# Hybrid mLSTM / neighbourhood-attention layer on one core: loading keys and queries four steps sooner, and weight splits ahead of the first tile's pieces

## The chip, the cores and the metric

The kernel runs on one core of a Trainium2 chip. The metric is the time of one execution on the device in microseconds (us), the median of several runs. Inputs and weights are in HBM, all in fp32.

## The reference

One layer over 2048 tokens of width 1024. Three token mixers run on one RMS-normalised input; their outputs are projected, gated, merged and added to the residual stream; an MLP with squared ReLU follows.

```python
def hybrid_layer(x, mem, ...):
    h = rmsnorm(x, g_mix)
    z = h @ w_in                                  # 1024 x 5648
    qk_m, v_m, o_m, i_pre, f_pre, qkv_na, q_mem, gate_pre = jnp.split(z, ...)
    # 1. bidirectional chunkwise mLSTM on conv(qk_m), v_m and the gates
    # 2. neighbourhood attention: 32 x 64 grid, window 8 x 16, 8 heads of 32
    h_na = neighbourhood_attention(rmsnorm(q_na), rmsnorm(k_na), v_na, rpb)
    # 3. cross-attention into 256 memory tokens
    h_mem = memory_cross_attention(q_mem, rmsnorm(mem, g_mem), w_mem_kv, ...)
    y = gates[0]*(h_m @ w_proj_mlstm) + gates[1]*(h_na @ w_proj_na) + gates[2]*(h_mem @ w_proj_mem)
    x = x + y @ w_out
    u = rmsnorm(x, g_ffn) @ w_up
    return x + jnp.square(jax.nn.relu(u)) @ w_down
```

## The kernel before

**Products.** Every large product is made of three fp32r matmuls (`mm3`, L242 to L244): each operand is kept as a high part and a low part, and high x high, high x low and low x high are summed in PSUM. A weight unit of 512 KB is loaded into a raw tile (`wr`, three buffers, issued by SP), then split: ScalarE writes the high part (L185), VectorE the low part (L186), into one of five `ws` buffers. `take` fetches units some steps ahead of their use (`self.ahead`, 5). `self.later` moves the splits of a unit back in the scheduler's order.

**Stages.** Phase 1 goes over four blocks of 512 tokens. It projects the normalised input `hT` to everything that the mixers need, and runs both attentions beside it. Phase 2 runs the mLSTM beside the gate projections. Phase 3 merges, projects and does the MLP. The order on TensorE is written out by hand; the other engines' orders come from a list scheduler that goes by priority. `queued(marks)` lets the instructions inside it be scheduled only behind the marked instructions.

**The beginning.** `mem_setup` projects the 256 memory tokens (PSUM tiles `mx`, weights from the first four units). While it runs, the first token tiles are loaded and normalised: ScalarE squares a tile of 128 x 1024 (L350), GpSimd makes the reciprocal root (L335, L336), VectorE scales (L352). TensorE then transposes a tile in two groups of four squares (L358, PSUM tiles `tr`), and each of the eight pieces is evicted twice into `hT`: ScalarE writes the high part (L363), VectorE the low part (L364). The first block has its four tiles in the order 2, 3, 0, 1; here they are called the first to the fourth tile. A tile's projection to neighbourhood queries and keys (PSUM `mm`, evicted as `zna`, L522) is eight steps of three matmuls; step k needs piece k of the tile, and the weight unit of steps 2i and 2i+1. The units of the first tile are called here the first to the fourth. The first tile's transposes run inside the projection of the memory tokens, those of the others inside the projection of the tile ahead of each: after its fourth and sixth step in the first tile, after the second and fourth in the second and third.

Beside this, `rms_x` (L462) squares the four tiles of the next block on ScalarE, `mem_rms` the memory tokens, `na_qk` (L964 to L971) normalises the keys and queries of a tile with VectorE and GpSimd, and GpSimd's result for the memory tokens is used by VectorE in L1232 and L1233.

**Key and query loads.** Neighbourhood attention works on units (four token rows, a group of four heads, a half of the columns). The two halves of a pair share the tiles `naq` and `nak`, two buffers each. `na_load_qk` issues six loads for a pair on SP (L1064, L1065), and is called by `na_unit` when the first half of the pair is set up, which happens as soon as the unit before it has done its first head (one head per step). Scores of a head are one matmul, L1110.

Of the kernel before, what the change touches and what calls it, by code (L numbers as in the profile page):

```python
# [16 lines left out]
AF = mybir.ActivationFunctionType  # L17
# [5 lines left out]
D = 1024  # L23
# [16 lines left out]
WSP, WRAW, AHEAD = 5, 3, 5  # L40
# [43 lines left out]
class Body:  # L84
    def __init__(self, tc, a):
        self.tc, self.nc, self.a = tc, tc.nc, a
        self.n = 0
        self.later, self.ahead = LATER, AHEAD
        self.streams, self.qkq, self.memq, self.aux_end = [], [], [], False
        self.na_ready, self.na_end, self.na_rate, self.tk = [], False, 1, 0  # L90
        self.na_v, self.na_vfree, self.scored = [], 2, False
        self.jobs, self.out, self.split = [], (), ()
        self.wplan, self.wready = self.plan(), []

# [905 lines left out]
    def na_stream(self):  # L1000


        todo, fetched, prev, ready = [], [], [], []
        biases, freed = [], [0] * NAB
        cur = last = None
        late = False
        while True:
            while self.na_ready:
                g = self.na_ready.pop(0)
                todo += [(g, hg, half) for hg in range(2) for half in range(2)]  # L1010
            if todo and not fetched and (cur is None or cur["h"] > 0):
                last = self.na_unit(*todo.pop(0), last, 4 if cur else 8)
                fetched.append(last)
                biases += [(last, h) for h in range(4)]
            if cur is None and not fetched and self.na_end and not prev and not ready:
                return
            if self.tk % 2:
                due = ready.pop(0)[1] if ready and ready[0][0] >= NA_VALUES and not self.scored else None
                if due and (self.na_rate == 2 or late):
                    self.na_values(due)  # L1020
                    due, late = None, False
                late = bool(ready and ready[0][0] >= NA_VALUES)
                self.scored = False
                step = self.tk == 3 or self.na_rate == 2
                if step and prev and prev[0][0] >= NA_LATER:
                    u, h, sb = prev.pop(0)[1]
                    self.na_transpose(u, h, sb)
                    if h == 3:
                        ready.append([0, u])
                if due:  # L1030
                    self.na_values(due)
                if step:
                    if cur is None and fetched and fetched[0]["wait"] <= 0:
                        cur = fetched.pop(0)
                    if cur:
                        while len(cur["bias"]) <= cur["h"]:
                            self.na_bias(*biases.pop(0))
                            freed.pop(0)
                        freed.append(3)
                        prev.append([0, self.na_scores(cur, cur["h"])])  # L1040
                        cur["h"] += 1
                        if cur["h"] == 4:
                            cur = None
            for u in fetched:
                u["wait"] -= 1
            for x in prev + ready:
                x[0] += 1

            freed = [max(n - 1, 0) for n in freed]
            if biases and freed and not freed[0]:  # L1050
                self.na_bias(*biases.pop(0))
                freed.pop(0)
            yield

    def na_load_qk(self, g, hg, kr0, nr):
        nc = self.nc
        q = self.p_a.tile([96, 4, 256], F32R, name=f"naq{g}_{hg}", tag="naq", bufs=2)
        k = self.p_a.tile([96, 4, 11 * 64], F32R, name=f"nak{g}_{hg}", tag="nak", bufs=2)
        qs = self.scr["qs"][:, g, hg].rearrange("(h d) l f t -> d h l (f t)", d=32)
        ks = self.scr["ks"][:, hg, :, kr0 * 64:(kr0 + nr) * 64].rearrange("(h d) l t -> d h l t", d=32)  # L1060

        for i, (lq, lk) in enumerate(((0, 0), (0, 1), (1, 0))):
            ds = slice(32 * i, 32 * i + 32)
            nc.sync.dma_start(q[ds].bitcast(F32), qs[:, :, lq])  # L1064
            nc.sync.dma_start(k[ds, :, :nr * 64].bitcast(F32), ks[:, :, lk])  # L1065
        return q, k

    def na_unit(self, g, hg, half, before, wait):

        nc = self.nc  # L1070
        kr0 = min(max(4 * g - 4, 0), 24)
        nr = 8 if g in (0, 7) else 11
        u = dict(g=g, hg=hg, half=half, nk=nr * 40, pts=[], h=0, wait=wait)
        u["qk"] = before["qk"] if half else self.na_load_qk(g, hg, kr0, nr)
        u["kts"] = [(3 * i, min(3, nr - 3 * i)) for i in range((nr + 2) // 3)]
        u["ho"] = before["ho"] if half else self.t("nho", [128, 2, 256], 1, F32R)
        u["bias"] = []
        self.na_v.append(u)
        self.na_load_v()
        return u  # L1080
# [75 lines left out]
    def mem_setup(self):  # L1156
        nc, a, p_a = self.nc, self.a, self.p_a


        warm = self.ps("mx")  # L1160
        for _ in range(9):
            nc.tensor.matmul(warm[:, 0:128], self.ones, self.ones, start=True, stop=True)
        gm = p_a.tile([128, 8], F32, name="gmem")
        self.gmix = p_a.tile([128, 8], F32, name="gmix")
        nc.scalar.dma_start(gm, a["g_mem"])
        mT = p_a.tile([128, 4 * 704], F32, name="memT", tag="nak", bufs=2)[:, :2 * D].rearrange("p (k t) -> p k t", k=8)
        later, self.later = self.later, 0
        for k in range(0, 8, 2):
            if k == 0:
                self.fetch(2)  # L1170
            (nc.sync if k else nc.scalar).dma_start(mT[:, k:k + 2], a["memT"][k * 128:(k + 2) * 128].rearrange("(k p) t -> p k t", p=128))
            for i in (k, k + 1):
                hi, lo, g = self.hT[:, 0, i, 0:256], self.hT[:, 1, i, 0:256], gm[:, i:i + 1]
                nc.scalar.activation(hi, mT[:, i], AF.Copy, scale=g)
                nc.vector.scalar_tensor_tensor(lo, mT[:, i], g, hi.bitcast(F32), ALU.mult, ALU.subtract)
            if k:
                self.fetch()
            if k == 2:
                nc.sync.dma_start(self.gmix, a["gT_mix"])
                self.prep_x()  # L1180
        self.prep_x()
        self.later = 0
        with self.queued(self.square):
            self.fetch()
        first = self.split
        self.later = 120
        self.fetch()
        second = self.split
        w = self.take(4)
        self.later = later  # L1190
        xs = p_a.tile([128, 4 * 704], F32, name="xstage", tag="nak", bufs=2)
        gq = p_a.tile([128, 2], F32, name="gmqk_raw")
        nc.sync.dma_start(gq, a["g_mem_qk"])
        self.gmqk = p_a.tile([128, 2], F32, name="gmqk")
        nc.vector.tensor_scalar(self.gmqk[:, 0:1], gq[:, 0:1], 0.125, None, ALU.mult)
        nc.vector.tensor_copy(self.gmqk[:, 1:2], gq[:, 1:2])
        self.mk = p_a.tile([128, 2, 2, 256], F32R, name="mk")
        self.mv = p_a.tile([128, 2, 256], F32, name="mv")
        ps = [self.ps("mx") for _ in range(2)]
        self.trans_x(MEM_T)  # L1200
        turns = self.jobs[-2:]

        def turn(f, marks):
            with self.queued(marks()):
                f()
        self.jobs[-2:] = [lambda f=f: turn(f, lambda: first) for f in turns]
        self.jobs += [lambda i=i: turn(lambda: self.prep_x(xt=xs[:, i * D:(i + 1) * D]), lambda: self.turned + second) for i in range(2)]
        for k in range(8):
            wk = w[k // 2]
            for t in range(2):  # L1210
                self.mm3(ps[t], self.lhs_tok(self.hT, k, t), (wk[:, 0, k % 2], wk[:, 1, k % 2]), k == 0, k == 7)
            self.tick()
        self.memz = []
        for t, p in enumerate(ps):
            z = self.t("zm", [128, 256], 4)
            nc.scalar.activation(z, p[:, 0:256], AF.Copy)
            nc.vector.tensor_copy(self.mv[:, t], p[:, 256:512])
            self.memz.append(z)

    def mem_rms(self):  # L1220
# [468 lines left out]
```

## Time and profile before

| what | value |
|---|---|
| median of 3 runs | 2863.81 us (2863.42 to 2864.61) |
| the profiled execution's own time | 2865.11 us |
| its span, first to last instruction | 2863.4 us |
| TensorE busy | 2844.4 us, 99% of the span |
| VectorE, ScalarE, GpSimd busy | 2046.7, 1163.9, 199.0 us |
| mean granted TensorE clock | 0.999 |

Times in the profile are microseconds from the span's start; PE is TensorE, DVE VectorE, ACT ScalarE, POOL GpSimd, SP the engine that issues most DMAs (SPq its queue). A row of the timeline gives start, duration, engine, line, operation, tile written and tiles read, the count, and in brackets how long the engine sat idle before it and what ended that. A row of the waits gives the total, the number of times and the longest.

### The profile page before, as it was taken

The numbers are of one execution on the slowest core, as the hardware profiler recorded it, in microseconds if no ns is written. First come the engines' busy times: TensorE is split into PE (matmuls) and PEld (weight loads), VectorE is DVE, ScalarE is ACT, GpSimd is POOL, SyncE is SP. The second block draws the span as 40 slices with busy tenths as digits, with TensorE's granted clock in tenths as the row PEclk, the third lists the DMA queues.
The fourth block names the chain that finished last, engine by engine and source line by source line (L and its number), as shares of the span: only waits on it lengthen the run. The fifth ranks groups of instructions, "written<-read, shape, count | busy, mean of one in ns | idle before, by whom it ended". The sixth has DMA issues, their size and how long they took to land.

```text
span 2863.4 us, 41480 instructions
## 1 busy us (share of the span) xinstructions
PE 2844.4 (99%) x14950; PEld 2355.7 (82%) x14950; DVE 2046.7 (71%) x3522; ACT 1163.9 (41%) x2205; POOL 199.0 (7%) x254
## 2 busy tenths in 40 slices
PE   9999999999999999999999999999999999999999
PEld 7888888888887888888888888888888888888887
DVE  7686865477765555647699888866786998887666
ACT  6464654355544433532343334333223433343331
POOL 3221210011000122310000000000000000000000
PEclk9999999999999999999999999999999999999999
DMA  8686777886899888977444447756773444476553
GB/s 294 210 281 208 248 238 245 263 245 204 281 312 310 266 271 265 308 262 267 121 152 149 149 162 244 242 196 229 256 219 121 152 149 149 162 249 230 196 188 133
DMA packets 345149, 631.70 MB, mean 221 GB/s; under 512 B 29584, under 2 KB 151376, under 8 KB 344944
## 3 DMA queue, kind: packets, MB, share of 16 engines
q1 hardware_dynamic: 344528, 628.79, 66.9%
q8 instruction: 118, 1.93, 0.3%
q14 instruction: 87, 0.71, 0.1%
q10 hardware_dynamic: 416, 0.27, 0.0%
HBM read 452.32 MB, written 176.62 MB: 220 GB/s over the span
## 4 chain that ended last, share of the span: by engine, by line
PE 92%; DVE 3%; DMA 2%; issue 1%; ACT 1%; POOL 0%; SPq 0%; ACTq 0%; DVEq 0%; POOLq 0%
PE mm L242 28%; PE mm L244 27%; PE mm L243 27%; PE tr L1130 2%; DMA wr<-in_w_units_dram 1%; PE pn L902 1%; PE mx L1144 1%; PE mx L1110 1%; PE pn L905 1%; PE mx L911 1%; PE mx L1305 1%; PE tr L1295 1%; PE mx L1275 1%; DVE ws L186 0%; DVE cy L707 0%
## 5 line engine op out<-in xcount | busy, mean ns | idle before, releaser
L242 PE MATMUL mm<-X,ws 128*128 128x512 f32 x896 | 349.5, 390 | 0.2 <-ACT u L1499 0.2
L243 PE MATMUL mm<-X,ws 128*128 128x512 f32 x896 | 348.6, 389 | 0.0
L244 PE MATMUL mm<-X,ws 128*128 128x512 f32 x896 | 348.6, 389 | 0.0
L186 DVE TENSOR_TENSOR ws<-wr,ws 128x1024 fp32r<-128x1024 f32 (+2 forms) x195 | 237.5, 1225 | 124.3 <-ACT ws L185 122.7
L242 PE MATMUL mm<-hT,ws 128*128 128x512 f32 (+1 forms) x776 | 304.8, 393 | 1.4 <-DMA hT<-s_hT 1.4
L244 PE MATMUL mm<-hT,ws 128*128 128x512 f32 (+1 forms) x776 | 301.7, 389 | 0.0
L243 PE MATMUL mm<-hT,ws 128*128 128x512 f32 (+1 forms) x776 | 301.4, 388 | 0.0
L185 ACT ACTIVATE ws<-wr 128x1024 fp32r<-128x1024 f32 (+2 forms) x195 | 204.6, 1055 | 192.6 <-PE mm L244 135.7
L244 PE MATMUL mm<-X 128*128 128x512 f32 x616 | 239.7, 389 | 0.5 <-DVE X L1563 0.5
L242 PE MATMUL mm<-X 128*128 128x512 f32 x616 | 239.7, 389 | 0.0
L243 PE MATMUL mm<-X 128*128 128x512 f32 x616 | 239.6, 389 | 0.0
L242 PE MATMUL mm<-ws,hT 128*128 128x512 f32 (+2 forms) x640 | 226.4, 354 | 2.7 <-ACT ws L185 1.6
L212 ACT ACTIVATE ws<-wr 128x512 fp32r<-128x512 f32 x224 | 133.9, 627 | 232.8 <-PE mm L244 145.6
L243 PE MATMUL mm<-ws,hT 128*128 128x512 f32 (+2 forms) x640 | 223.3, 349 | 2.1 <-DVE ws L186 2.1
L244 PE MATMUL mm<-ws,hT 128*128 128x512 f32 (+2 forms) x640 | 223.6, 349 | 0.1
L1562 ACT ACTIVATE X<-X 128x1024 fp32r<-128x1024 f32 x109 | 115.7, 1062 | 209.4 <-DMA X<-s_s 92.5
L242 PEld LDWEIGHTS mm<-X,ws 128*128 128x128 f32 x896 | 168.2, 188 | 36.0 <-ACT u L1499 0.6
L243 PEld LDWEIGHTS mm<-X,ws 128*128 128x128 f32 x896 | 168.2, 188 | 35.3 <-issue 0.5
L244 PEld LDWEIGHTS mm<-X,ws 128*128 128x128 f32 x896 | 168.2, 188 | 34.8
L1579 DVE TENSOR_TENSOR acc<-acc,mm 128x512 f32<-128x512 f32 x192 | 126.3, 682 | 70.0 <-PE mm L244 70.0
L1563 DVE TENSOR_TENSOR X<-X 128x1024 fp32r<-128x1024 f32 x109 | 132.4, 1222 | 58.0 <-ACT X L1562 57.4
L242 PEld LDWEIGHTS mm<-hT,ws 128*128 128x128 f32 x776 | 146.1, 188 | 31.0 <-issue 2.8
(280 smaller groups left out, 5946.1 us busy)
## 6 DMA issues: line engine op xcount, KB each, us to landing
wr<-in_w_units_dram SPq DMA_DIRECT2D x289, 512.0 KB
s_s<-u SPq DMA_DIRECT2D x32, 1024.0 KB
s_g<-ev SPq DMA_DIRECT2D x96, 256.0 KB
ev<-s_g SPq DMA_DIRECT2D x96, 256.0 KB
s_a<-u SPq DMA_DIRECT2D x96, 256.0 KB
X<-s_s SPq DMA_DIRECT2D x45, 512.0 KB
nab<-in_rpb_dram SPq DMA_DIRECT2D x96, 220.0 KB
xt<-in_w_units_dram SPq DMA_DIRECT2D x32, 512.0 KB
```

The source lines that it names most:

```text
L185: s = nc.scalar.activation(w[:, 0, ks], raw[:, ks], AF.Copy)
L186: v = nc.vector.tensor_tensor(w[:, 1, ks], raw[:, ks], w[:, 0, ks].bitcast(F32), ALU.subtract)
L212: nc.scalar.activation(hi, src, AF.Copy)
L242: mm(out, lhs[0], rhs[0], start=first, stop=False)
L243: mm(out, lhs[0], rhs[1], start=False, stop=False)
L244: mm(out, lhs[1], rhs[0], start=False, stop=last)
L902: mm(pn[h % 2][:, h // 2], pt[:, h], v1[:, h], start=h < 2, stop=first)
L905: mm(pn[h % 2][:, h // 2], qw[hp, h // 2], C[hp, h // 2], start=False, stop=True)
L1130: nc.tensor.transpose(ptp[0:120, j], sb[:, j * 120:(j + 1) * 120], self.ident)
L1562: nc.scalar.activation(hi, src, AF.Copy)
L1563: nc.vector.tensor_tensor(lo, src, hi.bitcast(F32), ALU.subtract)
L1579: nc.vector.tensor_tensor(c, first[t] if first else c, p, ALU.add)
```

## The change

Two parts. First, the key and query loads of the next pair are issued as soon as the first half of the present pair has done its first head, and kept in a table until its unit is set up; before, they were issued when the second half of the present pair had done its first head. That is four heads, or four steps, sooner.

Second, in `mem_setup`: the split of the sixth unit (the second of the first token tile) comes behind the split of the fifth in the scheduler's order; the pieces of the first token tile come behind both; `self.ahead` is 3 there, so that the two units after these are not fetched at this place; one of them is fetched in the middle of the projection, behind the first tile's pieces; the squares of the third and fourth tile come behind that unit's split; and the evictions of the memory projection (`zm`, `mv`) come behind the first tile's pieces. Nothing is computed otherwise, and the order on TensorE stays as it was.

```diff
@@ na_stream
+            nxt = [x for x in todo if x[2] == 0][:1]
+            if nxt and nxt[0] not in self.na_keys and cur and not cur["half"] and cur["h"] > 0:
+                self.na_keys[nxt[0]] = self.na_load_qk(*nxt[0][:2])
             if todo and not fetched and (cur is None or cur["h"] > 0):
                 last = self.na_unit(*todo.pop(0), last, 4 if cur else 8)
@@ na_unit
-        u["qk"] = before["qk"] if half else self.na_load_qk(g, hg, kr0, nr)
+        u["qk"] = before["qk"] if half else self.na_keys.pop((g, hg, half), None) or self.na_load_qk(g, hg)
@@ mem_setup
         first = self.split
         self.later = 120
-        self.fetch()
+        with self.queued(first):
+            self.fetch()
         second = self.split
+        self.ahead = 3
         w = self.take(4)
+        self.ahead = AHEAD
         self.later = later
...
-        turns = self.jobs[-2:]
+        turns, marks = self.jobs[-2:], list(first + second)
...
-        self.jobs[-2:] = [lambda f=f: turn(f, lambda: first) for f in turns]
-        self.jobs += [lambda i=i: turn(lambda: self.prep_x(xt=xs[:, i * D:(i + 1) * D]), lambda: self.turned + second) for i in range(2)]
+        self.jobs[-2:] = [lambda f=f: turn(f, lambda: marks) for f in turns]
+        preps = [lambda i=i: self.prep_x(xt=xs[:, i * D:(i + 1) * D]) for i in range(2)]
+        def last():
+            turn(turns[1], lambda: marks)
+            turn(self.fetch, lambda: self.turned)
+            marks.extend(self.turned + self.split)
+        self.jobs[-1:] = [last]
+        self.jobs += [lambda f=f: turn(f, lambda: marks) for f in preps]
@@ mem_setup, the evictions of the memory projection
-            nc.scalar.activation(z, p[:, 0:256], AF.Copy)
-            nc.vector.tensor_copy(self.mv[:, t], p[:, 256:512])
+            with self.queued(self.turned):
+                nc.scalar.activation(z, p[:, 0:256], AF.Copy)
+                nc.vector.tensor_copy(self.mv[:, t], p[:, 256:512])
```

Three stretches of the orders show what moves. The first is ScalarE around the last piece of the first token tile. Before (`tr_380` holds pieces of the first tile, here its last one, `tr_474` of the second; `ws_296`, `ws_301` and `ws_306` are the second to fourth unit, `ws_311` is a unit for later; `xstage` are the squares of the third and fourth tile):

```order
L363 ACTIVATE hT<-tr_380,gmix 128x128
L185 ACTIVATE ws_296<-wr_295 128x2x512
L350 ACTIVATE ev_400,sm_401<-xstage 128x1024
L185 ACTIVATE ws_301<-wr_300 128x2x512
L350 ACTIVATE ev_461,sm_462<-xstage 128x1024
L363 ACTIVATE hT<-tr_474,gmix 128x128
L185 ACTIVATE ws_306<-wr_305 128x2x512
```

And now, from the same last piece on, ScalarE (`tr_370` holds it, `tr_474` and `tr_493` the second tile's pieces, `ws_384` is the fourth unit and `ws_429` the one for later; ahead of these rows stand the splits of the second and, after the first two pieces, of the third unit):

```order
L363 ACTIVATE hT<-tr_370,gmix 128x128
L1230 ACTIVATE zm_402<-mx_313 128x256
L1230 ACTIVATE zm_405<-mx_314 128x256
L185 ACTIVATE ws_384<-wr_383 128x2x512
L350 ACTIVATE ev_395,sm_396<-xstage 128x1024
L350 ACTIVATE ev_461,sm_462<-xstage 128x1024
L363 ACTIVATE hT<-tr_474,gmix 128x128
L363 ACTIVATE hT<-tr_493,gmix 128x128
L185 ACTIVATE ws_429<-wr_428 128x8x128
```

All splits of the first tile's units now stand ahead of the two squares, and both squares stand ahead of every piece of the second tile.

The second place is ScalarE at the fourth tile (`tr_581` and `tr_600` hold its pieces, `xt_768` and `xt_784` are the third and fourth tile of the next block, squared by `rms_x`). Before, the square of `xt_784` stood behind the fourth tile's last piece (the second row here) and three weight splits:

```order
L462 ACTIVATE xt_768,sm_716<-xt_768 128x1024
L363 ACTIVATE hT<-tr_600,gmix 128x128
L522 ACTIVATE zna_626<-mm_574 128x512
L964 ACTIVATE sq_677<-zna_572 128x512
L185 ACTIVATE ws_434<-wr_433 128x8x128
L185 ACTIVATE ws_439<-wr_438 128x8x128
L1244 ACTIVATE sq_686<-zm_407 128x4x64
L185 ACTIVATE ws_444<-wr_443 128x8x128
L462 ACTIVATE xt_784,sm_716<-xt_784 128x1024
```

Now the two squares stand close to each other on ScalarE:

```order
L363 ACTIVATE hT<-tr_581,gmix 128x128
L462 ACTIVATE xt_768,sm_716<-xt_768 128x1024
L363 ACTIVATE hT<-tr_581,gmix 128x128
L363 ACTIVATE hT<-tr_600,gmix 128x128
L462 ACTIVATE xt_784,sm_716<-xt_784 128x1024
```

Both squares now stand inside the fourth tile's pieces, ahead of five of the eight.

The third place is SP at the last pair of neighbourhood units. Before, its loads stood behind the values (`nav_0_1`) and the last bias (`nab_0_1_3`) of the unit before it:

```order
L182 DMA wr_9747<-in_w_units_dram 128x1024
L1094 DMA nav_0_1_9856<-s_vna 120x2x128
L1095 DMA nav_0_1_9856<-s_vna 80x128
L105 DMA s_hna<-nho_9194 256x1x256
L1101 DMA nab_0_1_3_9878<-in_rpb_dram 128x320
L1064 DMA naq_1_9886<-s_qs 32x4x256
L1065 DMA nak_1_9887<-s_ks 32x4x512
```

Now they stand behind the last bias of the half before that one (`nab_0_0_3`), and ahead of a weight unit:

```order
L1105 DMA nab_0_0_3_9711<-in_rpb_dram 128x320
L1069 DMA naq_1_9719<-s_qs 32x4x256
L1070 DMA nak_1_9720<-s_ks 32x4x512
L1069 DMA naq_1_9719<-s_qs 32x4x256
L1070 DMA nak_1_9720<-s_ks 32x4x512
L1069 DMA naq_1_9719<-s_qs 32x4x256
L1070 DMA nak_1_9720<-s_ks 32x4x512
L182 DMA wr_9654<-in_w_units_dram 128x1024
```

The six loads moved up in SP's queue past four biases, two value loads, two weight units, two loads for the sums of down weights and five stores.

More of the change, by code (lines that the diff above doesn't have):

```diff
@@ L90, in __init__ @@
         self.na_ready, self.na_end, self.na_rate, self.tk = [], False, 1, 0
-        self.na_v, self.na_vfree, self.scored = [], 2, False
+        self.na_v, self.na_vfree, self.scored, self.na_keys = [], 2, False, {}
         self.jobs, self.out, self.split = [], (), ()
@@ L1053, in na_stream, with na_load_qk @@
             yield
-    def na_load_qk(self, g, hg, kr0, nr):
+    def na_load_qk(self, g, hg):
         nc = self.nc
+        kr0 = min(max(4 * g - 4, 0), 24)
+        nr = 8 if g in (0, 7) else 11
         q = self.p_a.tile([96, 4, 256], F32R, name=f"naq{g}_{hg}", tag="naq", bufs=2)
@@ L1070, in na_unit @@
         nc = self.nc
-        kr0 = min(max(4 * g - 4, 0), 24)
         nr = 8 if g in (0, 7) else 11
         u = dict(g=g, hg=hg, half=half, nk=nr * 40, pts=[], h=0, wait=wait)
-        u["qk"] = before["qk"] if half else self.na_load_qk(g, hg, kr0, nr)
+        u["qk"] = before["qk"] if half else self.na_keys.pop((g, hg, half), None) or self.na_load_qk(g, hg)
         u["kts"] = [(3 * i, min(3, nr - 3 * i)) for i in range((nr + 2) // 3)]
```

## The prediction

> **What bounds the kernel now.** I read the page first, then the waits of TensorE, the timeline of the places where it waits, and the windows by stretch. The page's head says who sets the end.
>
> ```profile
> span 2863.4 us, 41480 instructions
> PE 2844.4 (99%) x14950; PEld 2355.7 (82%) x14950; DVE 2046.7 (71%) x3522; ACT 1163.9 (41%) x2205; POOL 199.0 (7%) x254
> ```
>
> TensorE is busy for all but 19.0 us of the span, so a change that adds no matmul and takes none away can only win what TensorE waits. The waits of TensorE, longest in total first (total, times, longest), are 13 rows:
>
> ```profile
> PE mm L243 <- DVE ws L186: 2.1, 3, 0.8
> PE mx L1110 <- DMA nak<-s_ks: 1.7, 1, 1.7
> PE mm L242 <- ACT ws L185: 1.6, 1, 1.6
> ...
> PE mm L242 <- ACT zif L546: 1.0, 2, 0.8
> ...
> PE mm L242 <- ACT u L1499: 0.2, 1, 0.2
> ```
>
> They sum to 13.6 us. The change aims at the second row (one load of keys) and at the first and third (splits that the first token tile waits for). Where these stand, by the timeline of TensorE:
>
> ```profile
> 20.57 0.39 PE L242 MATMUL mm<-ws,hT 128*128 128x512 f32 x1
> 23.68 0.49 PE L242 MATMUL mm<-ws,hT 128*128 128x512 f32 x1 [1.59 <-ACT ws L185]
> 24.94 0.80 PE L243 MATMUL mm<-ws,hT 128*128 128x512 f32 x1 [0.77 <-DVE ws L186]
> 30.77 0.50 PE L243 MATMUL mm<-ws,hT 128*128 128x512 f32 x1 [0.61 <-DVE ws L186]
> 91.29 0.39 PE L242 MATMUL mm<-ws,hT 128*128 128x272 f32 x1 [0.84 <-ACT zif L546]
> ```
>
> The first three waits, 2.97 us, lie in the first token tile. What that tile loses in all is seen in the windows, one row for each of the four tiles of the first block, then three for the stretch of conv and values:
>
> ```profile
> 20.57:32.04 11.47, 8.50 (x34) 6.22 (x32) 9.20 (x21) 9.26 (x20) 2.10 (x4) 0.85 0.60 190
> 32.04:38.45 6.41, 6.41 (x33) 5.29 (x32) 3.44 (x10) 5.58 (x14) 3.98 (x3) 1.00 1.02 393
> 38.45:45.25 6.80, 6.68 (x34) 5.21 (x33) 3.97 (x14) 5.16 (x14) 1.07 (x3) 1.00 0.51 162
> 45.25:50.69 5.44, 5.44 (x25) 4.46 (x24) 3.41 (x7) 5.44 (x11) 1.81 (x2) 1.00 0.91 311
> 60.00:70.00 10.00, 10.00 (x49) 8.27 (x48) 9.36 (x17) 3.43 (x7) 2.72 (x4) 1.00 0.99 331
> 70.00:80.00 10.00, 10.00 (x67) 9.25 (x67) 9.89 (x17) 5.28 (x10) 5.58 (x2) 1.00 0.94 296
> 80.00:90.00 10.00, 9.83 (x76) 9.08 (x75) 9.96 (x26) 3.76 (x10) 6.23 (x5) 1.00 0.62 205
> ```
>
> The columns are the stretch, its length, busy time of PE, PEld, DVE, ACT and POOL, the granted clock, the DMA share and GB/s. The fourth tile (24 matmuls, no transposes) takes 5.44, that is 0.227 a matmul; the second, with two groups of transposes, 6.41, so I count 0.4 for a group. The first takes 11.47: 5.06 more than the second, the waits and a clock of 0.85. But ScalarE is busy 25.4 of these 30.1 us. Moving its work about frees little of it, and TensorE needs each tile's pieces from it.
>
> **The change part by part.** *Keys.* The rows of the last pair: two heads of the half before, the last key load on SP's queue, and the wait.
>
> ```profile
> 848.35 0.39 PE L1110 MATMUL mx<-nak,naq 96*128 96x320 f32 x1
> 851.58 0.40 PE L1110 MATMUL mx<-nak,naq 96*128 96x320 f32 x1
> 853.21 0.43 SPq L1065 DMA_DIRECT2D nak<-s_ks  x1
> 860.90 0.38 PE L1110 MATMUL mx<-nak,naq 96*128 96x320 f32 x1 [1.70 <-DMA nak<-s_ks]
> ```
>
> A head takes 3.23, so four steps are 12.9 us: the load, which took 7.7 us from issue to use, would be in some 11 us early. The six loads go ahead of a weight unit on SP; that unit's turn comes about six issues of 0.43 later, 2.6 us, covered by units fetched five ahead. The gain lies between 0 (another transfer is late next) and 1.7; I take **1.7**, since no other scores wait for their keys in the trace.
>
> *First token tile.* Durations and landings:
>
> ```profile
> 2.17 0.47 SPq L182 DMA_DIRECT2D wr<-in_w_units_dram  x1
> 8.09 1.06 ACT L185 ACTIVATE ws<-wr 128x1024 fp32r<-128x1024 f32 x1 [1.10 <-DMA wr<-in_w_units_dram]
> 14.25 2.25 SPq L182 DMA_DIRECT2D wr<-in_w_units_dram  x2
> 15.85 1.06 ACT L185 ACTIVATE ws<-wr 128x1024 fp32r<-128x1024 f32 x1
> 23.66 1.23 DVE L186 TENSOR_TENSOR ws<-wr,ws 128x1024 fp32r<-128x1024 f32 x1 [0.47 <-ACT ws L185]
> 44.28 0.62 ACT L363 ACTIVATE hT<-tr,gmix 128x128 fp32r<-128x128 f32 x2 [0.16 <-DVE hT L364]
> 45.06 0.62 ACT L363 ACTIVATE hT<-tr,gmix 128x128 fp32r<-128x128 f32 x2 [0.16 <-DVE hT L364]
> ```
>
> The second unit is issued at 14.25; its split can start no sooner than 16.9, the end of the first unit's, and no later than 20.2 (5.92 from issue to use, as in the upper rows). I take 18.7. Then ScalarE has it at 19.8, VectorE at 21.0; the first pieces follow (lower half 21.3, its partner 21.5); the third unit's lower half ends at 22.7; and the other pieces, which alternate between ScalarE and VectorE at 0.78 a pair, end their lower halves at 22.9, 23.7 and 24.5. TensorE comes at 20.57, waits for these four, and ends the fourth step at 24.75. Two groups of transposes and twelve matmuls later, and 0.1 for the fourth unit's lower half (27.1), the tile ends at **28.4** instead of 32.04.
>
> *Second tile.* ScalarE goes on with the evictions of the memory projection, the fourth split (to 25.9) and two squares before any piece.
>
> ```profile
> 23.53 1.05 ACT L350 ACTIVATE ev<-xstage 128x1024 bf16<-128x1024 f32 x1
> 25.61 0.75 DVE L352 TENSOR_SCALAR xstage<-xstage,rs 128x1024 f32<-128x1024 f32 x1 [0.72 <-ACT ws L185]
> 33.53 0.69 DVE L966 TENSOR_REDUCE sm<-sq 128x16 f32<-128x512 f32 x1 [0.47 <-ACT sq L964]
> 39.73 0.35 DVE L1232 TENSOR_SCALAR zm<-zm,rs 128x256 f32<-128x256 f32 x1 [2.65 <-POOL rs L336]
> ```
>
> From a square's start to its scaling are 2.08. The second square starts at 26.9, so its scaling on VectorE runs from 29.0 to 29.7, and the first pieces' lower halves, behind it there, end at 30.0; a split for later (1.23) stands before the next, 31.7. Behind these, ScalarE has an eviction, a square of the memory tokens and the square for L966 between the pieces, so I have the fourth step's lower half at 34.9. TensorE, which came at 28.4, ends that step at 35.2, and the tile at 35.2 + 0.4 + 12 x 0.227 = **38.3**: the 3.6 us have gone to the second tile.
>
> *Third and fourth tile.* The chain from L966 over GpSimd to L1232 took 6.2 before; L966 now starts at 34.0, so L1232 at 40.2, 0.5 later than before, and two of the third tile's pieces stand behind it in VectorE's order as they did. That tile ends at about 45.5 (before 45.25). In the fourth, two squares stand ahead of five of its pieces.
>
> ```profile
> 42.06 1.89 SPq L482 DMA_DIRECT2D xt<-in_x_dram  x2
> 51.02 1.06 ACT L462 ACTIVATE xt<-xt 128x1024 f32<-128x1024 f32 x1
> ```
>
> The second was done at 51.02. Its load waits for the buffer that the square before it frees, at 42.5 by my count; with 3.7 us to land (I had 4.4 for the second weight unit, and the queue is emptier) its square runs at 46.2 to 47.3, the pieces of the third and fourth step come at 47.9 and 48.7, and the tile ends at 48.95 + 2.72 = **51.7**, 1.0 later than the 50.69 of before. Bounds: no loss if the load is in by 45, and with the 7.7 us that the key load took a tile end of 55.7, 5.0 later.
>
> *Conv and values, 50 to 92 us.* VectorE is busy 9.36, 9.89 and 9.96 of each 10 us there, and its backlog makes the waits of 0.17 and 0.84 (the L546 row, 1.0). Two of its waits ahead of this stretch shorten, since GpSimd now makes the next block's root ahead of a key norm:
>
> ```profile
> 55.48 0.69 DVE L471 TENSOR_TENSOR zna<-ident,rs 128x512 f32<-128x512 f32 x1 [2.28 <-POOL rs L336]
> 90.61 0.41 DVE L545 COPY zm<-mm 128x256 f32<-128x256 f32 x1
> ```
>
> So VectorE reaches L545 about 1 us sooner, TensorE gets there later, and both waits go; with the restart after each I count **1.3**. Bounds are 0 and 1.6.
>
> *The sum:* 1.0 later at the fourth tile, less 1.3, less 1.7: **2.0 us less**. The rest of phase 1 and part of phase 2 get other orders on SP, ScalarE and VectorE; TensorE's own order is the same. I bound what that does by the largest single wait of the table on each side, 1.7, and take nothing. The profiled execution takes 2865.11, 1.7 outside its span, and 1.3 more than the median; 2.0 off gives 2863.1 there, and **2861.8** as median.
>
> On the clock: in the first tile 0.85 was granted over a stretch in which TensorE's longest wait was 1.59. The Trainium skill, TensorE: Matmul & The Clock Gate, section on the HAM clock gate, says the clock halves after an idle window of about 3.4 us. The trace differs, since no wait here is so long and the clock fell. By the rule no wait of the changed start would slow the clock, and the sum stays; by the trace it may, but the tiles then wait for pieces anyway.
>
> **The rivals.** *The start's gain stays.* If the pieces of the second tile come in time (the squares land early in ScalarE's idle time, 4.7 us over these four tiles), the 3.6 us are kept, and VectorE's later stretch, fed sooner, moves with them: 3.6 + 1.0 (the L546 row) + 1.7 = 6.3 less, 2858.8 and as median 2857.5. For it speaks that the waits named are real; against it, the two squares ahead of all pieces.
>
> *Slower: the last square's load.* If that load takes as long as the key load did, TensorE is 5.0 late at the fourth tile; less 1.3 and 1.7 that is 2.0 more, 2867.1 and as median 2865.8. It decides from a landing at 48.2 on, 2.0 after the one I counted, where the sum of -2.0 is used up. For it: before, the square came at 51.02 and nothing shows when the load was in.
>
> *The key loads don't help.* They go sooner but the transfers that they pass on SP come late and hold TensorE as long: 0.3 less, 2863.5 as median. For it, two weight units are among the transfers passed; against it, units are fetched five ahead.
>
> **How the numbers follow.** Chances: forecast 0.50, start kept 0.22, slower 0.15, keys without gain 0.13. A measurement of this kernel can tell 0.2%, 5.7 us, from no change: faster needs less than 2858.1. That holds for a little over half of the second case, 0.13; slower needs over 2869.5, which only the far end of the third reaches, 0.04; the rest, 0.83, is within. The range reaches from a little beyond the second case to the third: 2856.8 to 2866.2.
>
> **What would show it.** Right: no wait at L1110; the first tile ends near 28.4 with waits below 1 us in its first four steps; TensorE waits for pieces (L363, L364) in the second tile and ahead of the fourth tile's third step; conv starts between 50.5 and 52; no wait for L546 near 90. Wrong: conv starts at 47 to 48 (the second case), or after 53 (the third); a new wait of over 2 us anywhere behind 100 us would break the sum.

## The result, and the profile after

| | before | after |
|---|---|---|
| median | 2863.96 us (2863.42 to 2865.30, 5 runs) | 2890.18 us (2889.35 to 2892.23, 5 runs) |
| ratio after to before | 1 | 1.009, 95% interval 1.0078 to 1.0101 |
| profiled execution's own time | 2865.11 us | 2890.5 us |
| its span, mean granted clock | 2863.4 us, 0.999 | 2888.8 us, 0.996 |

The kernel became slower by 26 us. The page's head after, span and engines:

```profile
span 2888.8 us, 41484 instructions
PE 2854.4 (99%) x14950; PEld 2361.0 (82%) x14950; DVE 2045.0 (71%) x3522; ACT 1163.3 (40%) x2205; POOL 203.2 (7%) x254
```

The same matmuls stand there in the same order, and VectorE and ScalarE have no more work than before. TensorE is busy 10.0 us longer, and the span holds 15.4 us more in which it isn't. Since TensorE's order is the same, each matmul can be set beside its twin and the lag read. It is 0.9 us at 92.5, 4.9 behind the site at 163, 8.5 behind 314, 14.1 behind 591, 17.1 behind 772, 18.7 behind 812, 17.6 at 878 (where the wait for keys is gone), 19.5 behind 884, 25.9 behind 946 and 25.9 at the end. So nearly all of it comes up between 95 and 960 us, at seven sites. The windows of that stretch (busy time of PE, PEld, DVE, ACT, POOL, then granted clock, DMA share, GB/s), before:

```profile
95.00:960.00 865.00, 860.52 (x5560) 717.05 (x5559) 573.35 (x1286) 441.98 (x938) 87.14 (x91) 1.00 0.80 256
```

and after:

```profile
95.00:960.00 865.00, 843.73 (x5443) 702.55 (x5442) 560.63 (x1268) 433.19 (x926) 91.75 (x93) 0.99 0.78 249
```

TensorE stands idle 21.3 us there instead of 4.5, which is 16.8 more. The lag grows by 25.0, so the same matmuls also take 8.2 us longer. Most of that is the clock: it is halved for 17.1 us, where it never was before (in four places; rows of two windows stand in the last section), TensorE works in 14.5 us of these, and half of that, 7.2, is lost. What ends TensorE's idle time there, after (total, times, longest):

```profile
PE mm L242 <- DMA hT<-s_hT: 5.7, 1, 5.7
PE mm L242 <- ACT ws L185: 3.3, 1, 3.3
PE mx L1148 <- DVE sm L1118: 3.2, 1, 3.2
PE mx L1114 <- DVE sm L1118: 2.9, 2, 1.6
PE mx L1289 <- ACT me L1296: 1.9, 2, 1.4
PE mx L1114 <- ACT me L1296: 1.6, 1, 1.6
...
```

These are the evictions of scores (L1118, L1114 before), exps of the memory attention (L1296, L1282 before), one weight split and one load of the normalised input. None of them is an instruction that the change edits. **At 314**, the timeline of SP, ScalarE, VectorE and TensorE after:

```profile
301.95 0.33 SPq L482 DMA_DIRECT2D xt<-in_x_dram  x1
307.88 1.06 ACT L462 ACTIVATE xt<-xt 128x1024 f32<-128x1024 f32 x1 [1.89 <-DMA xt<-in_x_dram]
309.41 0.65 ACT L1120 ACTIVATE nsb<-nsb,sm 128x440 f32<-128x440 f32 x1
313.01 0.60 DVE L1118 CUSTOM_DVE_ANT_0 nsb<-mx,nab 128x440 f32<-128x440 f32 x1
313.68 1.08 PE L1148 MATMUL mx<-npt,nav 120*32 120x128 f32 x32 [3.16 <-DVE sm L1118]
```

and the same instructions before:

```profile
296.52 0.33 SPq L482 DMA_DIRECT2D xt<-in_x_dram  x1
300.43 0.66 ACT L1116 ACTIVATE nsb<-nsb,sm 128x440 f32<-128x440 f32 x1 [0.81 <-DVE sm L1114]
301.61 1.06 ACT L462 ACTIVATE xt<-xt 128x1024 f32<-128x1024 f32 x1 [0.42 <-DMA xt<-in_x_dram]
305.18 1.08 PE L1144 MATMUL mx<-npt,nav 120*32 120x128 f32 x32
```

Before, ScalarE did the exp of a head and then the square of a tile of the next block. After, the square stands ahead of the exp, and its load, issued 0.5 us later against the lag of 4.9 there, takes 0.8 longer to the square's start: ScalarE sits 1.89 us in front of the square with the exp behind it. VectorE in turn has its eviction behind work that waits for ScalarE, and TensorE waits 3.16. **At 163** it is VectorE that does a weight's lower half, a scaling and two pieces of the next block ahead of the maxima of the memory scores; ScalarE's exps come late. **At 591** SP issues nothing for 9.8 us, since a store at its head (`s_t`) waits for VectorE; behind it stand a load of the next block's input, issued 13 us later than the lag explains, and the weight unit. On ScalarE the split of that unit stands behind a piece made from that load. SP, ScalarE and TensorE, after:

```profile
579.52 0.88 SPq L105 DMA_DIRECT2D s_t<-xt  x2
589.36 0.63 ACT L448 ACTIVATE hT<-xt 128x512 fp32r<-128x512 f32 x1 [2.04 <-DVE xt L431]
590.99 0.49 PE L242 MATMUL mm<-ws,hT 128*128 128x512 f32 x1 [3.33 <-ACT ws L185]
```

**At 946**, the largest, the order on SP is turned: the load of the normalised input stood ahead of a store and a weight unit, and now stands behind them. SP and TensorE, after:

```profile
936.00 0.32 SPq L105 DMA_DIRECT2D s_o<-ev  x1
938.35 0.33 SPq L182 DMA_DIRECT2D wr<-in_w_units_dram  x1
938.78 0.52 SPq L589 DMA_DIRECT2D hT<-s_hT  x1
945.76 0.66 PE L242 MATMUL mm<-hT,ws 128*128 128x384 f32 x1 [5.71 <-DMA hT<-s_hT]
```

and before:

```profile
915.13 0.52 SPq L589 DMA_DIRECT2D hT<-s_hT  x1
...
918.84 0.33 SPq L182 DMA_DIRECT2D wr<-in_w_units_dram  x1
...
921.94 0.41 PE L242 MATMUL mm<-hT,ws 128*128 128x384 f32 x1 [1.40 <-DMA hT<-s_hT]
```

After, the store waits 4.0 us for VectorE and the unit 2.0 for its buffer, and the load is issued 4.1 us later than the lag of 19.5 would have it. From there to its use it takes 7 us in both kernels. The wait grows by 4.3: SP's order, and what it waits for at its head, is all the difference. The sites at 772, 812 and 884 are not followed here.

**The start** went as predicted up to the second tile. Its windows, first and second tile, after:

```profile
20.56:28.84 8.28, 7.49 (x33) 5.05 (x32) 6.67 (x14) 7.07 (x17) 1.33 (x3) 1.00 0.83 284
28.84:41.02 12.18, 10.40 (x33) 7.14 (x32) 5.25 (x13) 7.82 (x19) 5.47 (x7) 0.72 0.78 263
```

The two waits for pieces in the second tile:

```profile
30.61 0.50 PE L244 MATMUL mm<-ws,hT 128*128 128x512 f32 x1 [1.16 <-DVE hT L364]
32.27 0.79 PE L244 MATMUL mm<-ws,hT 128*128 128x512 f32 x1 [0.51 <-DVE hT L364]
```

The first tile ends at 28.84. The second waits for pieces, as forecast, but the clock is then halved for 6.83 us (0.72 in the row), so it ends at 41.02. The third ends at 47.44 and the fourth at 53.07, both with TensorE at work throughout. At 92.5 the lag is down from 2.4 to 0.9, since the waits at L546 are gone.

### The profile page after: what moved, and what is told of

The parts are those of the page before. It is cut to its first block, busy times and chain, and to the rows that moved or that the text cites. A ratio compares the mean times of both kernels' runs of the same rounds, so it can differ in the third digit from the quotient of the medians.

```text
span 2888.8 us, 41484 instructions
## 1 busy us (share of the span) xinstructions
PE 2854.4 (99%) x14950; PEld 2361.0 (82%) x14950; DVE 2045.0 (71%) x3522; ACT 1163.3 (40%) x2205; POOL 203.2 (7%) x254
## 4 chain that ended last, share of the span: by engine, by line
PE 94%; DMA 2%; DVE 2%; ACT 1%; issue 1%; SPq 0%; DVEq 0%; ACTq 0%
PE mm L242 29%; PE mm L244 28%; PE mm L243 28%; PE tr L1134 2%; PE mx L1148 1%; PE pn L902 1%; PE mx L1114 1%; PE pn L905 1%; PE mx L911 1%; PE mx L1319 1%; PE tr L1309 1%; DMA xt<-in_x_dram 0%; DVE ws L186 0%; DMA wr<-in_w_units_dram 0%; PE mx L1289 0%
```

## Theories

- **A, the orders.** The sooner loads change the scheduler's order of instructions that are none of their business, on ScalarE, VectorE and SP, and these orders make the new waits. A1: the computing engines' orders do it alone. A2: SP's order is needed as well.
- **B, the transfers.** The early loads themselves hold up others: at the head of SP's queue, or on the way.
- **C, the start.** The new start puts everything behind it out of step.
- **D, luck.** The old order was a tuned one, and any reordering of that size costs.

The compiled programs say this much beforehand: the start's part changes orders only up to about 92 us; the keys' part changes them behind that (in the traces from 115 us on for SP, from 130 us on for VectorE and ScalarE, and not only from 160, as the expectations have it), in 176 places on VectorE, 140 on SP, 119 on ScalarE, 5 on GpSimd and none on TensorE.

In several kernels orders are held. Each instruction of an engine gets an edge, without a semaphore, to the one that stood ahead of it in a recorded order; the scheduler then can't deviate, and nothing is added to the program:

```diff
+    def pin(self):
+        for engine, put in ORDERS.items():
+            mine = [i for i in todo if i.engine == engine and ... not in self.keyins]
+            order = [mine[n] for n in put]
+            for x, y in zip(order, order[1:]):
+                self.tc.add_manual_dep(y, x.name, NoSync)
```

`keyins` are the key and query loads, which the scheduler stays free to place around their call (in q_fix and q_fix2 they are held too). Medians stand beside the kernel before on the same chip (2865.87 to 2868.44 there, single runs some 8 us apart), so differences below about 4 us are read from the traces alone. Line numbers in these kernels are up to 24 higher.

## The experiments

**1. keys_only and start_only: each part of the change alone.** The first has the edits to `na_stream` and `na_unit`, the second those to `mem_setup`.

> The key and query loads four steps sooner, the beginning as before. Theory A (orders): calling the loads sooner changes the list scheduler's orders on ScalarE, VectorE and SP from 160 us on, and these orders make TensorE wait at nine places of phase 1; the start costs only its 0.9 us. So 2889 us (2863.96 + 26.2 - 0.9), with the waits of 3.2 us at L1148 near 313, 3.3 at L242 near 590 and 5.7 at L242 near 945. Theory B (transfers): the loads themselves hold up weight units and x pieces on SP's queue and the DMA engines: also 2889. Theory C (start): the later beginning pushes everything behind it out of step: 2862.3 (before, less the key wait of 1.7).

> The beginning of the changed kernel, the key loads as before. Theories A and B: 2864.9 us (2863.96 + 0.9, the lag of the changed kernel at 92 us), the first token tile done at 28.4, the second at 38.3 to 38.6, and the wait of 1.7 us for the keys back at L1110. Theory C: 2888 us, with the waits behind 160 us there.

Measured: the keys alone 2889.40 us, ratio 1.0081 (1.0066 to 1.0096), with the waits of after at the same places (2.1 at 163, 4.3 at 314, 6.3 at 949). The start alone 2871.74, ratio 1.0017 (1.0007 to 1.0026), a lag of 1.6 us at 92.5 and 2.4 in the span; by the medians it is 5.2 slower, and the profiled execution was the fastest of its ten. Its first two tiles:

```profile
20.39:31.61 11.22, 8.95 (x33) 6.33 (x32) 7.43 (x16) 7.83 (x17) 1.91 (x4) 0.85 0.86 276
31.61:39.97 8.36, 7.42 (x33) 5.04 (x32) 4.57 (x12) 7.07 (x19) 3.59 (x3) 1.00 0.90 298
```

Here the clock was halved in the first tile and not in the second. The edits are those of after, and where the slow stretch falls is not settled by them. C falls as the main cause: the waits behind 100 us come with the keys. But the start costs something too, where the prediction had a small gain.

**2. q_kb and q_bk: loads and orders crossed.** q_kb has the sooner loads and all other instructions of ScalarE, VectorE, GpSimd and SP in the order of before; q_bk has the loads at their old place and all others in the order of keys_only.

```diff
 q_kb: na_stream, na_unit as changed; ORDERS = those of before
 q_bk: na_stream, na_unit as before;  ORDERS = those of keys_only
```

> The key loads four steps sooner, the beginning as before, and every other instruction of ScalarE, VectorE, GpSimd and SP held in the order that it had before the change (an edge from each to the one ahead of it; the six loads of a pair are free to go where the scheduler puts them). Theory A: none of the nine waits; the 1.7 us wait for keys goes too: 2862.3 us. Theory B: the loads still pass weight units and x pieces on SP: 2889 us, or at least 2875.

> The reverse: the key loads called where they were before the change, and every other instruction of ScalarE, VectorE, GpSimd and SP held in the order that it has where the loads are called four steps sooner. Theory A: the nine waits without the early loads: 2889 to 2891 us (2889, and up to 1.7 for the keys). Theory B: 2864 us.

Measured: q_bk 2892.50, ratio 1.0090 (1.0075 to 1.0105), as slow as the whole change, with the loads called at their old place. Its waits between 95 and 960:

```profile
PE mm L250 <- DMA hT<-s_hT: 5.2, 1, 5.2
PE mx L1164 <- DVE sm L1134: 4.1, 1, 4.1
PE mx L1130 <- DMA nak<-s_ks: 3.2, 1, 3.2
...
```

The waits of after are there, and the wait for keys too. This is the run that decides: the orders are enough for the loss. One limit: the scheduler placed the loads anew among the others, and in five of the sixteen pairs the last load is issued 8 to 13 us sooner than before (the lag taken off). At 772 and 812 the loads are issued within 2 us of their old place and near 946 there are none, and the waits are there all the same. But q_kb isn't free either: 2879.10, ratio 1.0043 (1.0028 to 1.0057), as theory B has it at the least, with two new waits of 2.7 at 562 and 6.2 at 762 and 3.3 us of lag from smaller ones between 268 and 309. SP, ScalarE and TensorE there:

```profile
740.12 0.33 SPq L1089 DMA_DIRECT2D naq<-s_qs  x1
748.04 0.43 SPq L1090 DMA_DIRECT2D nak<-s_ks  x1
750.16 0.35 SPq L190 DMA_DIRECT2D wr<-in_w_units_dram  x1
759.48 1.06 ACT L193 ACTIVATE ws<-wr 128x1024 fp32r<-128x1024 f32 x1 [8.82 <-DMA wr<-in_w_units_dram]
762.38 0.73 PE L1134 MATMUL mx<-nak,naq 96*128 96x440 f32 x1 [6.21 <-DVE sm L1138]
```

The first of the six loads stands 4.3 us at SP's head, since its buffer is still read by scores; that costs little, for the store behind it waits for VectorE until 740.24 anyway. The issues of the other five fill 745.26 to 748.47, and SP waits 1.7 more, so the weight unit behind them is issued 4.9 us late (736.87 before, with a lag of 8.4 then). It takes 9.3 us from issue to split, where it took 5.2 at most before (split at 742.06). So B is real too, but none of after's sites is a wait for a unit behind such loads: at 591, where a unit is late, it stands behind a store.

**3. q_kcmp and q_bdve: which orders.** q_kcmp has the sooner loads and the computing engines' orders held to before, with SP free. q_bdve has the loads at their old place and VectorE alone in the order of keys_only.

```diff
 q_kcmp: ORDERS = those of before, without SP's
 q_bdve: ORDERS = VectorE's of keys_only
```

> Key loads four steps sooner; ScalarE, VectorE and GpSimd held in the order of before; SP free, so that the scheduler sorts all of its transfers around the early loads. Theory A1 (the orders of the computing engines carry the loss): within 3 us of before less the 1.7 of the keys, and no wait of over 2 us for VectorE or ScalarE behind 100 us. Theory A2 (SP's order carries it: early loads wait on SP for their buffer and hold the transfers behind them): 10 to 26 us slower than before, TensorE's waits ending on transfers or on the splits and pieces made of them.

> Key loads called where they were before the change; VectorE alone held in the order that it has where they are called sooner; ScalarE, GpSimd and SP free. Theory A1, with VectorE as the carrier: 2884 to 2892 us by the clock of the first runs (20 to 26 over before), with the waits at 161, 305 and 864 as in the changed kernel. Theory A2: less than 8 us over before.

Measured: q_kcmp 2898.55, ratio 1.0102 (1.0087 to 1.0118), with waits of its own at other places than after's, the longest 5.2 at 778 for an eviction of scores.

q_bdve 2902.55, ratio 1.0120 (1.0103 to 1.0137). Waits come at 163, 313, 590, 771 and 810 as in after, and bring the lag to 17.1 at 940. About as much again comes in phase 2, where VectorE's order doesn't fit the free engines' (one wait of 10.26 at 1097). Neither run isolates an engine. q_kcmp misses A1's forecast, and its 30 us are above A2's 10 to 26, with most waits ending on evictions and not on transfers; q_bdve misses A2's ("less than 8 us over before") and goes beyond A1's. The engines left free also didn't keep a known order: set beside each other from 95 to 1000 us, SP's order in q_kcmp differs from keys_only's about as much as from that of before, and so does ScalarE's in q_bdve. And q_kcmp has the sooner loads, which cost 12.6 in q_kb. What the two show is that VectorE's new order brings after's waits at five of the seven sites with the loads called at their old place, and that mixed sets of orders are as slow as the new one. Which engines are needed stays open between A1 and A2.

**4. p_shift6: other orders, no load moved.** The place of the early loads raises the scheduler's counter by as much as six loads do, and `na_unit` lowers it again.

```diff
+                self.tc.cur_priority += 6    # na_stream
+        self.tc.cur_priority -= 6            # na_unit
```

> No load is moved. The scheduler's priority counter is raised by six at the place where the changed kernel calls the six loads, and lowered by six at their old place; VectorE's order then differs in 25 places from 390 us on, against 176 from 160 us on. If the old order was merely a lucky one and any reordering costs (theory D): 3 to 10 us slower, with new waits between 390 and 900 us. If only the orders that the early loads bring are bad: within 2 us of before.

Measured: 2866.68, ratio 0.9996 (0.9987 to 1.0005), span 2864.2. VectorE's order differs in 25 places and nothing is lost. So it isn't true that any reordering costs, but the change makes 176 places, and the mixed sets of experiment 3, which also moved many, were slow. For reorderings of that size D stays open.

**5. q_last: the gain without the loss.** Only the last pair's loads go sooner, the one pair whose keys TensorE waited for; all else is held to before.

```diff
+            if nxt and nxt[0] == (7, 1, 0) and nxt[0] not in self.na_keys ...
```

> Only the loads of the last pair go four steps sooner, the one pair whose wait showed (1.7 us); every other instruction of ScalarE, VectorE, GpSimd and SP is held in the order of before. Theories A1 and D: the wait at L1110 near 861 goes and nothing comes in its place: 1.7 us under before. Theory A2: the six loads hold up transfers behind them, and a wait of 1 to 6 us appears between 840 and 865.

Measured: 2866.45, ratio 0.9993 (0.9984 to 1.0003), span 2863.4. The wait is gone:

```profile
861.01 0.40 PE L1134 MATMUL mx<-nak,naq 96*128 96x320 f32 x1
```

The lag falls by 1.6 there and nothing takes its place, but the profiled span ends as before, and in the medians 1.7 of 2866 can't be told from nothing. It is the best version found, and it isn't shown to be faster. It also shows no cost of holding orders by itself.

**6. q_fix and q_fix2: mend the orders.** keys_only with its own orders held, except for 13 instructions (19 in q_fix2) that are moved past those that stood in their way at six of the seven sites (none at 772):

```diff
 q_fix, by keys_only's times:
+  161: two L1282 ahead of L431, four L1286 ahead of L448
+  310: L1120 ahead of L462;  314: L1118 ahead of L449
+  593: L185, L186 ahead of L448, L431
+  814: L1118 ahead of L1139; 885: L1118 ahead of L605
+  941: load of hT ahead of a store and a weight unit
 q_fix2, besides:
+  L1262 ahead of L449; L1118 (164) ahead of L1290; L546 (399) ahead of L185
+  weight unit (586) ahead of two stores; L1122, L1123 (887) ahead of two L605
```

> The kernel with the sooner key loads alone, every instruction of ScalarE, VectorE, GpSimd and SP (the loads too) held in that kernel's own order, except for 13 instructions moved a few places ahead of next-block work or of a waiting copy: near 161 the two maxima L1282 and four exponentials L1286 ahead of L431 and L448; near 313 the exponential L1120 ahead of the square L462 and the scores' L1118 ahead of L449; near 594 the split L185, L186 ahead of L448 and L431; near 814 L1118 ahead of the copy L1139; near 886 L1118 ahead of L605; near 949 the load of hT (L589) ahead of a store and a weight unit. Theory A (orders): the waits at these six places go or shrink below 1.5 us, and the lost half-clock stretches behind them: 15 to 22 us under the kernel with the sooner loads, 2867 to 2875 us. Theory A2 (the transfers come late, whatever the computing engines' order): the waits stay under another name, 2884 us or more.

> As the kernel with 13 instructions moved, and six more: near 162 the query eviction L1262 ahead of L449 and the scores' L1118 ahead of a reciprocal; near 399 the gate eviction L546 ahead of a split; near 586 the load of a weight unit ahead of the two stores of s_t, at which SP stands 9.5 us; near 886 the reciprocal and scaling L1122, L1123 ahead of two of the L605. Theory A: the waits that were left near 162 (1.0), 392 (1.3), 586 (2.1 and 0.8) and 882 (1.4) go, with the half-clock stretches behind the first and third: 6 to 10 us under the kernel with 13, a span of 2869 to 2873 us against 2878.9. Theory A2: the weight unit lands no sooner for being issued sooner, since the DMA engines are full; the wait near 586 stays and the span is 2875 us or more.

Measured: q_fix 2882.77, ratio 1.0057 (1.0039 to 1.0075), span 13.9 us under that of keys_only, a little less than A's 15 to 22. At 314, ScalarE has exp and square in the old order again, and TensorE doesn't wait:

```profile
305.51 0.66 ACT L1140 ACTIVATE nsb<-nsb,sm 128x440 f32<-128x440 f32 x1 [1.16 <-DVE sm L1138]
306.18 1.05 ACT L482 ACTIVATE xt<-xt 128x1024 f32<-128x1024 f32 x1
308.81 1.08 PE L1168 MATMUL mx<-npt,nav 120*32 120x128 f32 x32
```

The 6.3 at 949 fell to 1.6; of the 2.7 in front of the split at 594, 2.1 stayed, and so did the 1.6 at 772. q_fix2 reached 2879.24, ratio 1.0048 (1.0031 to 1.0065), only 2.0 more in the span where 6 to 10 were expected. What was aimed at went or shrank, and others came:

```profile
166.46 1.06 ACT L482 ACTIVATE xt<-xt 128x1024 f32<-128x1024 f32 x1 [3.14 <-DMA xt<-in_x_dram]
168.95 0.86 PE L1168 MATMUL mx<-npt,nav 120*32 120x128 f32 x24 [3.13 <-ACT me L1306]
```

A square that waits 3.14 us for its load now stops the exps behind it, as at 314 in after. So 14 to 16 of the 29 us that keys_only has in its span (2892.8 against 2863.4) hang on 13 to 19 instructions. The spans make this look larger than it is, since keys_only's profiled execution was the slowest of its four: by the medians, each beside before on its own chip, 22.9 us fell to 15.2 and 13.4. With the waits gone or shrunk where the moves were made, that shows A there. The rest moved on as other waits. Whether order or late transfers make those stays open.

**7. q_kpool: the same loads off SP.** q_kb with the six loads issued by GpSimd.

```diff
-            nc.sync.dma_start(...)      # the loads of na_load_qk
+            nc.gpsimd.dma_start(...)
```

> Key loads four steps sooner, all issued by GpSimd instead of SP; every other instruction of ScalarE, VectorE, GpSimd and SP held in the order of before. If the 12.6 us that sooner loads cost in the old orders come from their waiting at the head of SP's queue: no wait of over 2 us behind 100 us, 2862 to 2866 us. If they come from the loads' packets on the DMA engines: the waits of 2.7 near 562 and 6.2 near 762 stay, 2874 us or more.

Measured: 2872.46, ratio 1.0017 (1.0007 to 1.0027); of q_kb's 12.6 us, 4.9 are left (in the spans, 9.7 of 15.1). Neither forecast came out whole: both waits are still there, 2.2 at 560 and 3.6 at 758, but smaller. Two neighbouring weight units, the second behind the six loads on the way though not in the queue, each with its issue on SP and its split on ScalarE:

```profile
738.83 0.63 SPq L190 DMA_DIRECT2D wr<-in_w_units_dram  x1
743.57 0.61 SPq L190 DMA_DIRECT2D wr<-in_w_units_dram  x1
744.76 1.06 ACT L193 ACTIVATE ws<-wr 128x1024 fp32r<-128x1024 f32 x1 [0.20 <-DMA wr<-in_w_units_dram]
754.85 1.06 ACT L193 ACTIVATE ws<-wr 128x1024 fp32r<-128x1024 f32 x1 [5.99 <-DMA wr<-in_w_units_dram]
```

The first was split 5.9 us after its issue, the second 11.3 us after, with up to 1440 KB of keys and queries issued between 738.50 and 742.03. The second is issued 0.3 us late against before instead of 4.9. So their place in SP's queue was a good part of B's price; that the transfers are the rest is likely, but argued from this one unit.

**8. k_r240: sooner in the program, later in priority.** The loads are called at the new place, with a priority number 240 higher, so that they might slip in behind more urgent ones without changing the rest.

```diff
+                prio = self.tc.cur_priority
+                self.tc.cur_priority = prio + 240
                 self.na_keys[nxt[0]] = self.na_load_qk(*nxt[0][:2])
+                self.tc.cur_priority = prio
```

> The key loads called four steps sooner, but with a priority number 240 higher (later), and the scheduler's counter set back behind them. VectorE's order then differs from before in 81 places from 400 us on, against 176 from 160 us on. Theory A: no wait of the new kind ahead of 400 us; behind it a part of the loss, 2868 to 2880 us, as waits at block boundaries (near 440, 590, 920) if next-block work has gone ahead of scores there.

Measured: 2901.72, ratio 1.0115 (1.0100 to 1.0130), a miss. The loads came later than before the change, and scores waited for them (and once, 7.0, for a bias):

```profile
PE mx L1117 <- DMA nak<-s_ks: 18.5, 3, 8.2
```

It tells nothing on A or B, only that three key loads that come late cost more than the one wait that the change was after.

## Why the prediction was wrong

- **Keys, 1.7 less: right in itself.** After, the scores' matmul that waited runs without a wait, and the lag falls by 1.8 there (a new wait at 884 takes it back):

```profile
878.52 0.39 PE L1114 MATMUL mx<-nak,naq 96*128 96x320 f32 x1
```

- **The price of passing SP: mis-sized.** "that unit's turn comes about six issues of 0.43 later, 2.6 us, covered by units fetched five ahead" counts issues alone. In q_kb, where nothing else changes, the unit is issued 4.9 us later and then takes 9.3 us to its split instead of 5.2 at most. The cover of five units didn't hold. This costs 12.6 us with the old orders; how much of it is in after is not known.
- **First tile, 28.4: right (28.84).** Second tile, 38.3: the waits stood where I had them, but TensorE was idle for 1.8 (12.18 less 10.40) where I had 3.5 (9.9 for the tile less the 6.41 of before), and the end was 41.02. The halved clock cost about 3.4, and I had let the clock out because "the tiles then wait for pieces anyway"; the tile had matmuls to do as well. The waits that I had in the third and fourth tile (7.2 and 6.2 long) didn't come: with TensorE 2.7 later the pieces were there, and the tiles took 6.42 and 5.63. So they ended 1.9 and 1.4 late by two errors that partly cancel, which is luck. The waits at L546 went, worth 1.5 where I had 1.3. So the start ended 0.9 late instead of 0.3 early; in the other kernels with an unchanged start the lag at 92.5 lies between 0.5 early and 1.5 late, so little hangs on that.
- **The failed step:** "The rest of phase 1 and part of phase 2 get other orders on SP, ScalarE and VectorE; TensorE's own order is the same. I bound what that does by the largest single wait of the table on each side, 1.7, and take nothing." It is 26.8 us: the lag of 25.9, less 0.9 of the start, plus 1.8 of the keys. q_bk shows that such orders suffice for it. The bound was no bound. The waits in the table of before are those that the old orders left, so they say nothing of the waits that other orders make; and one wait was counted where there were seven sites, three of which halved the clock for 3.4 us and one for 6.8. The prediction's own sign of error ("a new wait of over 2 us anywhere behind 100 us") did appear, with waits of 5.7, 3.3 and 3.2.
- **The rivals:** none happened. The slower one put its price on one transfer of the start; the one on transfers held up on SP named what q_kb shows, with a price of 1.7 at most instead of 12.6.

## What to carry to other kernels

Where a list scheduler sets the order of the engines beside the bound one, moving six loads is an edit to every engine's order: compare the orders of the whole program, and price each place where an instruction that TensorE waits for falls behind one that waits for something else. Waits in the old profile don't bound this. The slack between producer and consumer at the moved places might; no run here tried that. When a gain rests on one site (here one wait of 1.7), move that one load and hold the rest: q_last lost nothing by it.

## What the runs showed of the hardware

**The clock goes by a fixed grid.** In each of the fourteen traces the clock changes at instants that are whole multiples of 3.413 us apart, with another offset in each execution. Windows of that grid in after, around the sites at 163 and 314:

```profile
161.84:165.25 3.41, 1.47 (x14) 1.11 (x14) 3.31 (x10) 3.01 (x11) 0.00 (x0) 1.00 0.82 276
165.25:168.66 3.41, 3.41 (x11) 2.82 (x11) 3.41 (x8) 2.42 (x7) 0.00 (x0) 0.50 0.52 169
308.61:312.02 3.41, 1.91 (x9) 1.25 (x7) 1.84 (x5) 2.55 (x7) 0.00 (x0) 1.00 0.47 110
312.02:315.43 3.41, 1.75 (x35) 1.46 (x36) 2.37 (x6) 2.29 (x7) 1.03 (x2) 1.00 0.98 343
315.43:318.84 3.41, 3.41 (x20) 2.92 (x20) 2.36 (x7) 2.53 (x9) 3.32 (x2) 1.00 0.80 255
```

At 163, waits of 1.41 and 0.53 lie in one window, TensorE is idle for 1.94 of its 3.41 us, and the next window has half the clock. At 314 a longer wait, 3.16, falls on two windows, 1.50 and 1.66, and the clock stays. Over all traces up to 1000 us, each of the 37 windows with 1.86 us or more of idle time was followed by a halved one, 5 of the 25 with 1.50 to 1.86, and one of the 43 with 0.90 to 1.50 that ran at full speed themselves. A halved stretch lasts one window or two, seldom more; what decides that is not seen here. So a window idle for over half costs 1.7 us or more in the next, and it is the luck of the offset whether a wait of 2 to 3.5 us makes one. The Trainium skill, TensorE: Matmul & The Clock Gate, section on the HAM clock gate, gives a free-running window of 3413 ns and wants an idle window of about 3.4 us for the slower state. The length and the free running agree with these rows; that the whole window must be idle does not, 1.94 was enough.

**A load's way and its place in the queue are two prices.** With six loads ahead of it on SP a weight unit was issued 4.9 us late and took 9.3 us from issue to split. With the loads issued by GpSimd it was issued 0.3 us late and took 11.3, where the unit ahead of it took 5.9; before the change it took 5.2 at most. The stand of 4.3 us at SP's head for a buffer moved the next issue by only 0.3, since the store there wasn't ready sooner either.
